# Widening block 1's narrow matmuls and transposes with zeros to the whole array

## The chip, the cores and the metric

The kernel runs on one core of a Trainium2 chip. The metric is the device time of one execution in microseconds (us): the median of three runs is given, and one further execution was profiled. TensorE's array has 128 rows and 128 columns; a matmul names the rows (partitions of its operands) and columns (of its weights) that it uses. In the rows below `64*128 64x272` means 64 rows and 128 columns of weights, and 272 columns that stream past them.

## What is computed

Two blocks work on 512 tokens of 1024 features. Only block 1 is touched. It has two layers over L = 528 tokens (16 learned ones ahead of the 512); each layer has a mixer of two branches, retention and attention, followed by a feed-forward part.

```
q_r, k_r, v_r, g_r, q_a, k_a, v_a, gate_r, gate_a = split(rms_norm(h) @ w_in)
# retention, 8 heads, 64 features to a key, 128 to a value, both directions
s = (q_c @ k_c.T) * decay_in          # within a block of 128 tokens
o = s @ v + q_dec @ state             # and over the blocks before and after
state = state * chunk_decay + k_dec.T @ v
# attention, 8 heads in 2 groups of 4, 64 features; a band of 3 blocks and the 16 first tokens
p = softmax([q @ meta_k.T, q @ k_band.T, sink]);  o = p @ [meta_v, v_band]
```

Block 2 (a gated delta rule, a linear recurrence, attention into a memory and product-key experts) follows and stays as it is.

## The kernel before

Products with weights are made in three passes of the type float32r, whose operands are split into a first part (`whi`, `uh`) and a rest (`wlo`, `ul`); they go through `gemm` (L263) in two halves of 264 tokens, or of 512 columns where layer 1 leaves the first tokens out. Other products are plain float32, which TensorE runs as two instructions to a matmul; so L767's four matmuls stand as eight in the trace. Transposes are matmuls against `ident`.

Phase A of a layer starts with the tokens' scales: sums of squares, a power on GpSimd (`rsqrt_small`, L222), transposes that spread it as rows (L375), then rope tables times these scales (L592, L593), the retention's queries and keys (L597 to L601) and the values, turned token-major by five transposes to a tile (L632). The first 16 tokens' values lie in `Vm`: the retention's in rows 0 to 15, the attention's (`VAm`) in rows 32 to 47, and, as eight small copies issued by ScalarE's queue (L657), in rows 64 to 127 again, block diagonal over the four heads of a group (`VMB`).

Then three generators are interleaved: `retention` (one head after another), `projections` (the remaining products with weights, in steps of 12 matmuls, which fill in) and `attention` (one block of queries and one group after another, two steps to a turn). They start in this order, and attention starts when its queries and keys are there. The order on each engine follows the order of this code and what the framework's scheduler makes of it.

Narrow products stand in these places:

- `scores`, L833 and L834: a head's scores are two products into the same place. `QS` holds a group's first parts in 64 rows and the rests in the other 64, `KH` the keys' first parts twice, so L833 uses all 128 rows. L834 multiplies the first parts with the keys' rests, `KL`, in the 64 rows of the group alone. Where the first 16 tokens do not lie beside the band, both are made once for 16 columns and once for the band.
- `turned`, L857, and `weighted`, L881: the weights over the first 16 tokens of four heads are turned (64 columns) and multiplied with `VMB` (64 rows).
- `retention`: L764 (16 columns), L765 (16 rows, 64 columns) and, among the outputs, L788 for the first block (16 rows, `Vm`).
- L632's first transpose to a tile, and L738 (16 columns).

Of the kernel before, what the change touches and what calls it, by code (L numbers as in the profile page):

```python
# [15 lines left out]
EPS = 1e-6  # L16
# [169 lines left out]
def _program(tc, I, out, dbg, upto, layers, pools):  # L186
# [26 lines left out]
    warm = cst.tile([128, 1], F32, name="warm")  # L213
    nc.scalar.activation(warm, ones, AF.Copy)
# [4 lines left out]
    def rsqrt_small(dst, src, scale):  # L219
        """dst = (src*scale + EPS)^-0.5 for a narrow [p, n]."""  # L220
# [6 lines left out]
    def load_w(src=None, sub=None, pool=None, into=None):  # L227
        """a tile of weights, as the sum of two that a pass each carries"""
# [85 lines left out]
    # ---------------------------------------------------------------- first block  # L314
# [42 lines left out]
    def cols6(acc, scale):  # L357
        """rsqrt(mean over partitions) per token, blocks of tokens as columns"""
# [8 lines left out]
    def bcast6(r6):  # L367
        """the same as rows, all partitions alike: slices of the tokens and where they are"""
# [26 lines left out]
    def cols(acc, scale, n):  # L395
        """rsqrt(mean over partitions) per token, [128, n/128]"""
# [7 lines left out]
    def bcast(r):  # L404
        """[128, k] -> rows [128, k*128] in PSUM, the same on all partitions"""
# [20 lines left out]
    # the memory's keys and values, a tile at a time where the first block leaves the tensor engine room  # L426
# [4 lines left out]
    mcol = cst.tile([128, 2], F32, name="mcol")  # L431
# [27 lines left out]
    def memory_values(ng, mem):  # L459
        """two steps"""  # L460
# [19 lines left out]
    # the first layer's input, and its first products  # L480
# [7 lines left out]
    def products_aside(feed_c, n, scale=1.0, fills=(), room=None):  # L488
        """the first four tiles of a phase, put aside until the tokens' scales are there"""
# [27 lines left out]
    for l in range(layers):  # L517
# [3 lines left out]
        # from here on the last layer leaves the first tokens out, except as keys and values  # L521
# [5 lines left out]
        # ============================================================ phase A  # L527
# [10 lines left out]
        # distances: between tokens of a block, and down a column to the block's ends  # L538
# [9 lines left out]
        nex = pa.tile([128, 16], F32, name="nex")  # L548
        nc.vector.tensor_scalar(nex, ex, -1.0, None, op0=OP.mult)
        # decays of a block's keys towards its end and its start, and of a whole block (of the sums from the  # L550
        # tokens before in the upper half, from those after in the lower)
# [6 lines left out]
        # what turns the distances' decays into those to a block's ends  # L558
        tdec = pa.tile([128, 2, 8], F32, name="tdec")
        for k in range(2):  # L560
            nc.vector.tensor_scalar(tdec[:, k], nex[:, 8 * k:8 * k + 8], dcol[:, 3 + k:4 + k], None, op0=OP.mult)
        # the tokens' scales as columns, for the blocks of TB
# [8 lines left out]
        Vx = R("R2", [128, 4, D], F32, "Vx")  # L571
        Vm = pa.tile([128, D], F32, name="Vm")
        VAx = pa.tile([128, 4, 128], F32, name="VAx")
        VAm = Vm[32:32 + NM, :128]
        # the attention's keys, split in two: the first parts of a group twice, the rests once
        KH = pa.tile([128, 2, L], F32R, name="KH")
        KL = pa.tile([128, L], F32R, name="KL")
        QO = R("R6", [128, 2, 4, L], F32, "QO")
        # a block of queries makes room for its own outputs; the other half holds what retention cycles through
        QA = OA = QO[:, 0]  # L580
        spare = QO[:, 1].rearrange("p a b -> p (a b)")
        # keys of one head of a chunk, with zeros for the other; a head's queries with both decays
# [7 lines left out]
        def scaled(tab):  # L590
            """a table times the tokens' scales"""
# [34 lines left out]
        # values, turned to token-major; the retention's minus their mean over a head's features, so that  # L626
        # its outputs have mean zero
        def values(m, z):
            pt, pm = PS(), PS()
            for i, (s0, n) in enumerate(TB):  # L630
                o = pm[:n, :128] if i == 0 else pt[:, 128 * i - 128:128 * i]
                nc.tensor.transpose(o, z[:, s0:s0 + n], ident)  # L632
# [19 lines left out]
        # the first tokens' values of a group, block diagonal over its heads  # L652
        VMB = Vm[64:, :512].rearrange("p (g d) -> p g d", g=2)
        nc.vector.memset(VMB, 0.0)
        for g in range(2):
            for r in range(4):
                nc.scalar.dma_start(VMB[16 * r:16 * r + 16, g, 64 * r:64 * r + 64], VAm[:, 64 * g:64 * g + 64])  # L657
# [11 lines left out]
        # ---- projections that fill in: queries and keys of the attention, then the retention's gates  # L669
        def projections():  # L670
            for c in range(5):
# [5 lines left out]
                else:  # L677
                    rope([(z, slice(0, 128))], z, rope_a, ROT_A)
                    for g in range(2):
# [3 lines left out]
                        nc.vector.tensor_tensor(KL[own], z[own], KH[own, g].bitcast(F32), op=OP.subtract)  # L683
# [11 lines left out]
        # ---- retention: within a block of tokens as it stands, between blocks by the decayed sums of keys  # L695
        # times values over the blocks before and after
        def retention():
# [35 lines left out]
            def turn(c):  # L733
                """a chunk's keys, token-major"""
# [3 lines left out]
                nc.tensor.transpose(pm[:NM, :128], QK[:, 1, c, :NM], ident)  # L738
                return pt, pm

            def decayed(h, pt, pm):
                f = slice(64 * (h % 2), 64 * (h % 2) + 64)
                kd = pa.tile([128, 576], F32, name="kd", tag="kd", bufs=2)
                k4, k0 = b4(kd[:, :512]), kd[:NM, 512:]
# [3 lines left out]
                nc.scalar.activation(k0, pm[:NM, f], AF.Copy, scale=kdec[:NM, 2, h:h + 1])  # L748
                return k4, k0
# [3 lines left out]
            for h in range(8):  # L753
# [5 lines left out]
                (k4, k0), S_, vh = kds[e], SD[e], slice(h * 128, h * 128 + 128)  # L759
# [8 lines left out]
                sT = pa.tile([128, L], F32, name="sT", tag="sT", bufs=1)  # L768
# [1190 lines left out]
```

## Time and profile before

| What | before |
|---|---|
| median of 3 runs | 3728.36 us (3717.03 to 3739.03) |
| span of the profiled execution | 3726.1 us |
| TensorE busy (its weight loads) | 3586.0 us, 96% (3212.1 us, 86%) |
| VectorE, ScalarE, GpSimd busy | 2413.2, 1494.8 and 946.7 us |
| mean granted TensorE clock | 0.976 of full speed |

The profiled execution gives its span, from the first to the last instruction; its own time is not listed apart from that, and the median of the runs lies 2.3 us above it. The ends of matmuls are modelled, so a busy TensorE need not be one that streams data all the time: the starts of successive matmuls tell more. Phase A's interleaved part lies at about 124 to 350 us in layer 0, and at about 1098 to 1300 us in layer 1; attention takes part from 184 and from 1160 us on.

### The profile page before, as it was taken

The numbers are of one execution on the slowest core, as the hardware profiler recorded it, in microseconds if no ns is written. First come the engines' busy times: TensorE is split into PE (matmuls) and PEld (weight loads), VectorE is DVE, ScalarE is ACT, GpSimd is POOL, SyncE is SP. The second block draws the span as 40 slices with busy tenths as digits, with TensorE's granted clock in tenths as the row PEclk, the third lists the DMA queues.
The fourth block names the chain that finished last, engine by engine and source line by source line (L and its number), as shares of the span: only waits on it lengthen the run. The fifth ranks groups of instructions, "written<-read, shape, count | busy, mean of one in ns | idle before, by whom it ended". The sixth has DMA issues, their size and how long they took to land. (4 is left out here: it accounts for less than half of the span.)

```text
span 3726.1 us, 54318 instructions
## 1 busy us (share of the span) xinstructions
PE 3586.0 (96%) x21341; PEld 3212.1 (86%) x21341; DVE 2413.2 (65%) x4258; ACT 1494.8 (40%) x2675; POOL 946.7 (25%) x708
## 2 busy tenths in 40 slices
PE   8999999999999999999999999997889999999998
PEld 8989999999997888788878877887778999999987
DVE  7554436333656454633467755689979988888875
ACT  4454324222444432422344453425553434434333
POOL 4211112000422111200032330446433334333321
PEclk9988999999998999999999999998999999999999
DMA  4101232222320033322232131323468878888855
GB/s 138 58 23 41 93 119 97 90 89 89 124 86 29 30 105 116 101 96 96 93 123 68 35 96 55 116 86 119 130 209 323 338 304 320 315 320 324 317 212 181
DMA packets 185887, 531.42 MB, mean 143 GB/s; under 512 B 16416, under 2 KB 70048, under 8 KB 168992
## 3 DMA queue, kind: packets, MB, share of 16 engines
q1 hardware_dynamic: 150272, 367.67, 29.6%
q0 software_dynamic: 18432, 134.23, 9.1%
q10 hardware_dynamic: 16928, 26.06, 2.1%
q8 instruction: 168, 2.75, 0.3%
q14 instruction: 87, 0.71, 0.1%
HBM read 492.64 MB, written 35.19 MB: 142 GB/s over the span
## 5 line engine op out<-in xcount | busy, mean ns | idle before, releaser
L243 ACT ACTIVATE whi<-wraw 128x1024 fp32r<-128x1024 f32 x594 | 627.6, 1058 | 1043.0 <-PE g L263 628.3
L244 DVE TENSOR_TENSOR wlo<-wraw,whi 128x1024 fp32r<-128x1024 f32 x543 | 680.5, 1254 | 294.9 <-ACT whi L243 287.6
L263 PE MATMUL g<-uh,whi 128*128 128x264 f32 (+1 forms) x1864 | 476.1, 318 | 4.6 <-ACT z L605 4.6
L263 PE MATMUL g<-uh,wlo 128*128 128x264 f32 (+1 forms) x1864 | 468.7, 314 | 1.3 <-DVE wlo L244 1.3
L263 PE MATMUL g<-ul,whi 128*128 128x264 f32 (+1 forms) x1864 | 468.8, 314 | 0.0
L350 POOL TENSOR_TENSOR ssq<-ssq,sq 128x512 f32<-128x512 f32 (+2 forms) x84 | 133.4, 1588 | 926.1 <-issue 715.8
L1721 PE MATMUL f<-TH,wlo 128*128 128x384 f32 x1024 | 348.8, 341 | 5.4 <-POOL wlo L244 5.4
L1721 PE MATMUL f<-TH,whi 128*128 128x384 f32 x1024 | 350.8, 343 | 1.2 <-ACT stash L1722 1.1
L1721 PE MATMUL f<-TL,whi 128*128 128x384 f32 x1024 | 347.5, 339 | 0.0
L263 PEld LDWEIGHTS g<-uh,whi 128*128 128x128 f32 x1864 | 308.4, 192 | 25.4 <-ACT z L605 5.0
L263 PEld LDWEIGHTS g<-uh,wlo 128*128 128x128 f32 x1864 | 307.7, 191 | 21.4 <-DVE wlo L244 1.6
L263 PEld LDWEIGHTS g<-ul,whi 128*128 128x128 f32 x1864 | 308.2, 191 | 19.6 <-issue 1.3
L1904 POOL COPY pace<-al 1x1 f32<-1x1 f32 x128 | 109.4, 855 | 563.6 <-DVE al L332 561.8
L1883 PE MATMUL acc<-whi,ah 128*128 128x512 f32 x768 | 240.1, 394 | 7.3 <-ACT whi L243 6.4
L1883 PE MATMUL acc<-wlo,ah 128*128 128x512 f32 x768 | 238.9, 392 | 4.1 <-DVE wlo L244 4.1
L1883 PE MATMUL acc<-whi,al 128*128 128x512 f32 x768 | 238.5, 392 | 0.0
L263 PE MATMUL g<-Hh,wlo 128*128 128x264 f32 (+1 forms) x768 | 203.9, 320 | 0.0
L263 PE MATMUL g<-Hl,whi 128*128 128x264 f32 (+1 forms) x768 | 203.8, 320 | 0.0
L263 PE MATMUL g<-Hh,whi 128*128 128x264 f32 (+1 forms) x768 | 203.4, 319 | 0.0
L1853 POOL DMA_INDIRECT gtile<-in_uv_dram,ix x128 | 189.8, 1483 | 46.4 <-issue 27.4
L1721 PEld LDWEIGHTS f<-TH,whi 128*128 128x128 f32 x1024 | 196.2, 192 | 5.8 <-ACT stash L1722 1.9
L1721 PEld LDWEIGHTS f<-TH,wlo 128*128 128x128 f32 x1024 | 195.5, 191 | 6.4 <-POOL wlo L244 6.4
(588 smaller groups left out, 7608.3 us busy)
## 6 DMA issues: line engine op xcount, KB each, us to landing
wraw<-in_w_dram SPq DMA_DIRECT2D x340, 512.0 KB, 3.5
wraw<-in_uT_dram SPq DMA_DIRECT2D x128, 512.0 KB, 5.6
wraw<-in_uv_dram SPq DMA_DIRECT2D x128, 512.0 KB, 4.9
gd<-stg SPq DMA_DIRECT2D x12, 2048.0 KB, 9.9
gin<-gd SPq DMA_DIRECT2D x32, 768.0 KB, 11.2
h0c<-in_h_dram SPq DMA_DIRECT2D x8, 264.0 KB, 4.3
H<-in_h_dram ACTq DMA_DIRECT2D x8, 264.0 KB, 5.9
hs<-H ACTq DMA_DIRECT2D x8, 264.0 KB, 2.1
```

Of the source, the lines that this page charges most:

```text
L243: nc.scalar.activation(hi, raw, AF.Copy)
L244: (sub or nc.vector).tensor_tensor(lo, raw, hi.bitcast(F32), op=OP.subtract)
L263: nc.tensor.matmul(pw, wt[:, sl], xt[:, kc, hf * w_:(hf + 1) * w_], start=(first and n == 0 and a == 0), stop=(last and n == len(kcs) - 1 ...
L350: nc.gpsimd.tensor_tensor(self.acc, self.acc, t, op=OP.add)
L1721: nc.tensor.matmul(p[:, :NT], wt[:, sl], x[:, kc], start=(kc == 0 and a == 0), stop=(kc == 7 and a == 2))
L1853: nc.gpsimd.indirect_dma_start(out=gtile, out_offset=None, in_=I["uv"], in_offset=bass.IndirectOffsetOnAxis(ap=ix[:, k:k + 1], axis=0))
L1883: nc.tensor.matmul(accs[2 * n + q], x[:, tk], wt[:, 512 * q:512 * q + 512], start=(j == 0 and k == 0), stop=(j == 127 and k == 2))
L1904: after = nc.gpsimd.tensor_copy(pace, ready[2][0:1, 0:1].bitcast(F32)).ins
```

## The change

Narrow operands are widened with zeros, so that the products use all 128 rows, and columns where it can be done, of the array. `KL` becomes two tiles, one for each group, with zeros in the other 64 rows (the second one takes the buffer of `ssq`). `Vm` is zeroed once and read in all its rows, against `K0`, `sT` and `pM`, which have zeros where they meet rows that belong to something else. `K0` takes the place of the part of `kd` that held the decayed keys of the first tokens; it holds both heads of a chunk side by side. `sams` are two tiles with zeros in columns 0 to 63 instead of one narrow tile. Transposes of 16 columns take 128. Some small tiles are merged (`warm`, `nex`); comments are removed, which shifts the line numbers.

```diff
         Vm = pa.tile([128, D], F32, name="Vm")
+        nc.gpsimd.memset(Vm, 0.0)
-        KL = pa.tile([128, L], F32R, name="KL")
+        KL = [pa.tile([128, L], F32R, name="KL"), wk.tile([128, L], F32R, name="KL1", tag="ssq", bufs=1)]
+        for t in KL:
+            nc.gpsimd.memset(t.bitcast(F32), 0.0)
+        sams = [pa.tile([128, 128], F32, name=f"sam{e}") for e in range(2)]
+        for e in range(2):
+            nc.gpsimd.memset(sams[e], 0.0)
+        nc.gpsimd.memset(K0, 0.0)
+        sT = pa.tile([128, L], F32, name="sT")
+        nc.gpsimd.memset(sT[:, :NM], 0.0)
...
-                o = pm[:n, :128] if i == 0 else pt[:, 128 * i - 128:128 * i]
-                nc.tensor.transpose(o, z[:, s0:s0 + n], ident)
+                o = pm[:, :128] if i == 0 else pt[:, 128 * i - 128:128 * i]
+                nc.tensor.transpose(o, z[:, s0:s0 + 128], ident)
...
-                        nc.vector.tensor_tensor(KL[own], z[own], KH[own, g].bitcast(F32), op=OP.subtract)
+                        nc.vector.tensor_tensor(KL[g][own], z[own], KH[own, g].bitcast(F32), op=OP.subtract)
...
-                nc.tensor.transpose(pm[:NM, :128], QK[:, 1, c, :NM], ident)
+                nc.tensor.transpose(pm[:, :128], QK[:, 1, c, :128], ident)
...
-                nc.scalar.activation(k0, pm[:NM, f], AF.Copy, scale=kdec[:NM, 2, h:h + 1])
+                nc.scalar.activation(K0[:NM, f], pm[:NM, f], AF.Copy, scale=kdec[:NM, 2, h:h + 1])
...
-                nc.tensor.matmul(px_[:NM, 128:128 + NM], KP[e][:, :NM], QK[:, 0, c, :NM], start=True, stop=True)
-                nc.tensor.matmul(px_[:64, :128], k0, Vm[:NM, vh], start=True, stop=True)
+                nc.tensor.matmul(px_[:, 128:128 + NM], KP[e][:, :128], QK[:, 0, c, :NM], start=True, stop=True)
+                nc.tensor.matmul(px_[:, :128], K0, Vm[:, vh], start=True, stop=True)
...
-                nc.scalar.activation(S_[:64, 1], px_[:64, :128], AF.Copy)
+                nc.scalar.activation(S_[:64, 1], px_[64 * e:64 * e + 64, :128], AF.Copy)
...
-                    nc.tensor.matmul(o, v_rows(b)[:n, vh], sT[:n, s0:s0 + n], start=True, stop=False)
+                    nc.tensor.matmul(o, v_rows(b)[:, vh], sT[:, s0:s0 + n], start=True, stop=False)
...
-                    nc.tensor.matmul(sp[:nq, a:a + n], QS[own, g, r], KL[own, b:b + n], start=False, stop=True)
+                    nc.tensor.matmul(sp[:nq, a:a + n], QS[:, g, r], KL[g][:, b:b + n], start=False, stop=True)
...
-            nc.gpsimd.tensor_copy(sam[:nq], sa[:nq, :, 0:16])
+            sam = sams[g]
+            nc.gpsimd.tensor_copy(sam[:nq, 64:].rearrange("p (r k) -> p r k", r=4), sa[:nq, :, 0:16])
...
-            nc.tensor.transpose(pm[:64, :nq], sam[:nq], ident[:nq, :nq])
+            nc.tensor.transpose(pm[:, :nq], sams[g][:nq], ident[:nq, :nq])
-            nc.vector.tensor_copy(pM[64:, :nq], pm[:64, :nq])
+            nc.vector.tensor_copy(pM[:, :nq], pm[:, :nq])
...
-            nc.tensor.matmul(po[:nq, :256], pM[64:, :nq], VMB[:, g], start=True, stop=False)
+            nc.tensor.matmul(po[:nq, :256], pM[:, :nq], VMB[:, g], start=True, stop=False)
```

The order of instructions moves in few places. Here is TensorE's at the start of layer 0's retention, head 0 (the shape is that of the result; L765 is the product of the first tokens' keys and values, L767 those of the blocks, L788 the first block's output). Before:

```order
L263 MATMUL g<-uh,wlo 128x264 x2
L767 MATMUL s<-Vx,kd 128x128
L765 MATMUL s<-Vm,kd 64x128
L767 MATMUL s<-Vx,kd 128x128 x3
L263 MATMUL g<-uh,whi 128x264 x2
L263 MATMUL g<-ul,whi 128x264 x2
```

And with the change, where L776 is what L765 was, and L778 what L767 was (`Vx` as its second name is `K0`, which lies in the same tile):

```order
L263 MATMUL g<-uh,wlo 128x264 x2
L778 MATMUL s<-Vx,kd 128x128 x4
L263 MATMUL g<-uh,whi 128x264 x2
L776 MATMUL s<-Vm,Vx 128x128
L263 MATMUL g<-ul,whi 128x264 x2
```

The product with `Vm` moved behind all four of the blocks and two of the filling matmuls, since it reads all rows of `Vm`.

GpSimd's order at the start of layer 1's phase A (L222 is the power of the tokens' scales, the SD tiles are the retention's sums). Before:

```order
L543 IOTA dcol 128x1 x5
L588 MEMSET SD_10308 128x640
L222 TENSOR_TENSOR r_10244<-r_10244,mhalf 88x6
L588 MEMSET SD_10309 128x640
L593 TENSOR_TENSOR rope_r<-rope_r,rsb 128x528
```

And with the change:

```order
L542 IOTA dcol 128x1 x5
L574 MEMSET Vm 128x1024
L222 TENSOR_TENSOR r_10236<-r_10236,mhalf 88x6
L581 MEMSET KL 128x528
L581 MEMSET KL_10299 128x528
L585 MEMSET sam_10302 128x128
L585 MEMSET sam_10303 128x128
L589 MEMSET sT 128x16
L600 MEMSET SD_10311 128x640
L600 MEMSET SD_10312 128x640
L605 TENSOR_TENSOR rope_r<-rope_r,rsb 128x528
```

`Vm`'s memset stands where one of SD's stood, and five more stand between the power and the rope table's scaling, beside both of SD's.

## Rows read from the trace of the kernel before

**Rows 1.** The page: the span.

```profile
span 3726.1 us, 54318 instructions
```

**Rows 2.** Busy time by stretch: retention alone and with attention, layers 0 and 1.

```profile
core 0: us, PE busy (x) PEld busy (x) DVE busy (x) ACT busy (x) POOL busy (x), PEclk, DMA share, GB/s
124.00:184.00 60.00, 56.22 (x468) 53.15 (x466) 37.23 (x78) 24.38 (x66) 22.34 (x16) 1.00 0.16 51
184.00:350.00 166.00, 165.55 (x1055) 141.15 (x1056) 79.25 (x244) 79.33 (x192) 23.85 (x26) 0.86 0.07 23
1098.00:1160.00 62.00, 59.31 (x459) 55.66 (x458) 37.52 (x75) 23.47 (x63) 21.37 (x16) 0.94 0.15 51
1160.00:1300.00 140.00, 138.43 (x770) 109.06 (x770) 72.12 (x209) 72.03 (x168) 20.80 (x24) 0.89 0.07 22
```

**Rows 3.** TensorE's waits, 184 to 350 us: total, times, longest.

```profile
PE s L833 <- ACT KH L682: 1.5, 1, 1.5
```

**Rows 4.** TensorE's timeline, 233.4 to 237 us: start, duration, engine, line, operation.

```profile
233.40 0.42 PE L263 MATMUL g<-uh,wlo 128*128 128x264 f32 x2
233.65 0.34 PE L833 MATMUL s<-KH,QS 128*128 128x400 f32 x1
...
234.30 0.45 PE L833 MATMUL s<-KH,QS 128*128 128x400 f32 x1
234.68 0.45 PE L834 MATMUL s<-KL,QS 64*128 64x400 f32 x1
235.06 0.45 PE L833 MATMUL s<-KH,QS 128*128 128x400 f32 x1
```

**Rows 5.** TensorE's timeline, 219 to 222 us.

```profile
219.54 0.59 PE L833 MATMUL s<-KH,QS 128*128 128x272 f32 x1
220.06 0.59 PE L834 MATMUL s<-KL,QS 64*128 64x272 f32 x1
...
221.19 0.64 PE L263 MATMUL g<-ul,whi 128*128 128x264 f32 x2
221.63 0.64 PE L263 MATMUL g<-uh,wlo 128*128 128x264 f32 x2
```

**Rows 6.** The tile KL: its products, count and forms.

```profile
L834 PE MATMUL s<-KL,QS x104: 273/386/699, 184.8 to 1281.0; 64*128 64x16 f32 x32, 64*128 64x272 f32 x16, 64*128 64x400 f32 x16, 64*128 64x384 f32 x16
```

**Rows 7.** TensorE's timeline, 130 to 138 us, without the lines of L263.

```profile
130.78 0.43 PE L765 MATMUL s<-Vm,kd 16*64 16x128 f32 x2
...
135.01 0.43 PE L765 MATMUL s<-Vm,kd 16*64 16x128 f32 x2
135.36 0.94 PE L767 MATMUL s<-Vx,kd 128*128 128x128 f32 x6
136.13 0.29 PE L789 MATMUL g<-QO,SD 128*128 128x16 f32 x2
136.28 0.47 PE L788 MATMUL g<-sT,Vx 128*128 128x128 f32 x2
```

**Rows 8.** The tile Vm: its products, and its copies from issue to landing.

```profile
L881 PE MATMUL s<-Vm,pM x36: 376/480/792, 199.0 to 1297.9; 64*128 64x256 f32 x32, 64*16 64x256 f32 x4
L765 PE MATMUL s<-Vm,kd x32: 267/293/318, 130.8 to 1266.5; 16*64 16x128 f32 x32
L788 PE MATMUL g<-sT,Vm x32: 257/278/392, 132.6 to 1286.0; 16*128 16x16 f32 x32
...
DMA to landing us min/median/max: 1.6/1.8/2.2
```

**Rows 9.** GpSimd's groups by form: busy us, mean ns.

```profile
L585 POOL MEMSET QO<- 128x2112 f32 x2 | 3.7, 1867 | 3.9 <-DVE tn L1046 3.9
```

**Rows 10.** TensorE's timeline, start of layer 1's phase A.

```profile
1010.11 0.67 PE L375 MATMUL s<-ident,r 88*128 88x88 f32 x6 [1.05 <-POOL r L222]
```

**Rows 11.** ScalarE's timeline, issues of the copies into Vm.

```profile
126.21 3.18 ACTq L657 DMA_DIRECT2D Vm<-Vm  x5
```

**Rows 12.** Busy time by stretch, around a fall of the clock (columns as in rows 2).

```profile
199.40:202.80 3.40, 3.40 (x29) 2.64 (x29) 2.14 (x8) 2.34 (x4) 1.31 (x1) 1.00 0.02 5
...
216.50:223.30 6.80, 6.80 (x25) 5.37 (x24) 2.54 (x12) 1.87 (x5) 1.50 (x2) 0.50 0.00 1
```

More of the change, by code (lines that the diff above doesn't have):

```diff
@@ L212, in _program @@
     nc.vector.memset(ones, 1.0)
-    warm = cst.tile([128, 1], F32, name="warm")
-    nc.scalar.activation(warm, ones, AF.Copy)
+    mcol = cst.tile([128, 2], F32, name="mcol")
+    nc.scalar.activation(mcol[:, 0:1], ones, AF.Copy)
     mhalf = cst.tile([128, 8], F32, name="mhalf")
@@ L430, in _program @@
     ghead = cst.tile([128, 8], F32, name="ghead")
-    mcol = cst.tile([128, 2], F32, name="mcol")
     mrow = []
@@ L547, in _program @@
             nc.scalar.activation(ex, ex, AF.Exp)
-        nex = pa.tile([128, 16], F32, name="nex")
-        nc.vector.tensor_scalar(nex, ex, -1.0, None, op0=OP.mult)
+        nex = pa.tile([128, 8], F32, name="nex")
+        nc.vector.tensor_scalar(nex, ex[:, :8], -1.0, None, op0=OP.mult)
         kdec = pa.tile([128, 4, 8], F32, name="kdec")
@@ L560, in _program @@
         for k in range(2):
-            nc.vector.tensor_scalar(tdec[:, k], nex[:, 8 * k:8 * k + 8], dcol[:, 3 + k:4 + k], None, op0=OP.mult)
+            nc.vector.tensor_scalar(tdec[:, k], ex[:, 8 * k:8 * k + 8], dcol[:, 3 + k:4 + k], -1.0, op0=OP.mult, op1=OP.mult)
         rcol = pa.tile([128, 5], F32, name="rcol")
@@ L570, in _program @@
         QK = R("R3", [128, 2, 4, L], F32, "QK")
-        Vx = R("R2", [128, 4, D], F32, "Vx")
+        Vx_ = R("R2", [128, 4 * D + 128], F32, "Vx")
+        Vx, K0 = Vx_[:, :4 * D].rearrange("p (b d) -> p b d", b=4), Vx_[:, 4 * D:]
         Vm = pa.tile([128, D], F32, name="Vm")
+        nc.gpsimd.memset(Vm, 0.0)
         VAx = pa.tile([128, 4, 128], F32, name="VAx")
@@ L651, in _program @@
         values(*turned_)
-        VMB = Vm[64:, :512].rearrange("p (g d) -> p g d", g=2)
-        nc.vector.memset(VMB, 0.0)
+        VMB = Vm[:, :512].rearrange("p (g d) -> p g d", g=2)
+        nc.vector.memset(VMB[64:], 0.0)
         for g in range(2):
             for r in range(4):
-                nc.scalar.dma_start(VMB[16 * r:16 * r + 16, g, 64 * r:64 * r + 64], VAm[:, 64 * g:64 * g + 64])
+                nc.scalar.dma_start(VMB[64 + 16 * r:80 + 16 * r, g, 64 * r:64 * r + 64], VAm[:, 64 * g:64 * g + 64])
         rope_a = pa.tile([128, 2, L], F32, name="rope_a", tag="rope")
@@ L742, in decayed @@
                 f = slice(64 * (h % 2), 64 * (h % 2) + 64)
-                kd = pa.tile([128, 576], F32, name="kd", tag="kd", bufs=2)
-                k4, k0 = b4(kd[:, :512]), kd[:NM, 512:]
+                k4 = b4(pa.tile([128, 512], F32, name="kd", tag="kd", bufs=2))
                 src = pt.rearrange("p (b d) -> p b d", b=4)[:, :, f]
@@ L747, in decayed @@
                 nc.scalar.activation(k4[:, :, 64:], src, AF.Copy, scale=kdec[:, 1, h:h + 1])
-                nc.scalar.activation(k0, pm[:NM, f], AF.Copy, scale=kdec[:NM, 2, h:h + 1])
-                return k4, k0
+                nc.scalar.activation(K0[:NM, f], pm[:NM, f], AF.Copy, scale=kdec[:NM, 2, h:h + 1])
+                return k4
             T = prepare(0)
@@ L758, in retention @@
                     yield
-                (k4, k0), S_, vh = kds[e], SD[e], slice(h * 128, h * 128 + 128)
+                k4, S_, vh = kds[e], SD[e], slice(h * 128, h * 128 + 128)
                 st, px_, pu = PS(), PS(), PS()
@@ L763, in retention @@
                                      start=True, stop=True)
-                nc.tensor.matmul(px_[:NM, 128:128 + NM], KP[e][:, :NM], QK[:, 0, c, :NM], start=True, stop=True)
-                nc.tensor.matmul(px_[:64, :128], k0, Vm[:NM, vh], start=True, stop=True)
+                nc.tensor.matmul(px_[:, 128:128 + NM], KP[e][:, :128], QK[:, 0, c, :NM], start=True, stop=True)
+                nc.tensor.matmul(px_[:, :128], K0, Vm[:, vh], start=True, stop=True)
                 for b in range(4):
                     nc.tensor.matmul(pu[:, 128 * b:128 * b + 128], k4[:, b], Vx[:, b, vh], start=True, stop=True)
-                sT = pa.tile([128, L], F32, name="sT", tag="sT", bufs=1)
                 nc.vector.tensor_tensor(b4(sT[:, NM:]), b4(st), T[:, None, :].to_broadcast([128, 4, 128]), op=OP.mult)
                 nc.vector.tensor_mul(sT[:NM, :NM], px_[:NM, 128:128 + NM], T[:NM, :NM])
-                nc.scalar.activation(S_[:64, 1], px_[:64, :128], AF.Copy)
+                nc.scalar.activation(S_[:64, 1], px_[64 * e:64 * e + 64, :128], AF.Copy)
                 nc.scalar.activation(S_[64:, 3], pu[64:, 384:], AF.Copy)
@@ L815, in scores @@
             q0, nq = TB[qb]
-            own = slice(64 * g, 64 * g + 64)
             if qb == 0:
@@ L848, in scores @@
             nc.vector.reciprocal(den, den)
-            sam = wk.tile([128, 4, 16], F32, name="sam", tag="sam", bufs=1)
-            nc.gpsimd.tensor_copy(sam[:nq], sa[:nq, :, 0:16])
-            return qb, g, ot, kb, sa, den, sam
+            sam = sams[g]
+            nc.gpsimd.tensor_copy(sam[:nq, 64:].rearrange("p (r k) -> p r k", r=4), sa[:nq, :, 0:16])
+            return qb, g, ot, kb, sa, den
         def turned(u):
-            qb, g, ot, kb, sa, den, sam = u
+            qb, g, ot, kb, sa, den = u
             q0, nq = TB[qb]
             pm = PS()
-            nc.tensor.transpose(pm[:64, :nq], sam[:nq], ident[:nq, :nq])
+            nc.tensor.transpose(pm[:, :nq], sams[g][:nq], ident[:nq, :nq])
             pM = wk.tile([128, 128], F32, name="pM", tag="tm", bufs=3)
-            nc.vector.tensor_copy(pM[64:, :nq], pm[:64, :nq])
+            nc.vector.tensor_copy(pM[:, :nq], pm[:, :nq])
             pTs = []
@@ L876, in weighted @@
         def weighted(u, pM, pTs):
-            qb, g, ot, kb, sa, den, sam = u
+            qb, g, ot, kb, sa, den = u
             q0, nq = TB[qb]
```

## The prediction

> **What bounds the kernel now.** I read the page's span first, then a table of stretches, then the waits of TensorE, then the timeline of TensorE inside those stretches. The profiled execution spans 3726.1 us [rows 1]; the median of the three runs, 3728.36, lies 2.3 us above it, so I take the sum off the median. The change touches only phase A of both layers of block 1: the retention alone, and then retention, attention and the filling projections in turns. There the reader is to see two things in the stretches [rows 2]. TensorE counts as busy nearly all the time (165.55 of 166 us in layer 0, 138.43 of 140 in layer 1), while VectorE and ScalarE are each busy for about half (79.25 and 79.33 of 166). And the granted clock falls to 0.86 and 0.89 in the attention stretches and to 0.94 in layer 1's retention. TensorE has one wait of 1.5 us in the whole 166 us of layer 0's attention [rows 3]. So TensorE's own order sets the end there: what is taken off it comes off the time until VectorE or ScalarE cannot follow.
>
> Busy is not useful, though. In the timeline, two matmuls of 264 columns over the whole array start 0.25 us apart as a pair, 0.125 each. Scores run as KH (128 rows), KL (64 rows), KH, KL; each has 400 columns, so by columns each should take 0.19. They start 0.38 apart, in both directions [rows 4]. The 0.19 us over belongs to each passage between a 128-row and a 64-row product; an ordinary change of weights, as between the 264-column products, has no such gap. At half the clock the same pattern of 272 columns takes 0.52 a product, where two of 264 take 0.44 together, 0.22 each: 0.29 over [rows 5, 12].
>
> **The change part by part.**
>
> *The rests of the scores (KL).* There are 104 such products, 32 of 16 columns [rows 6]; each has a passage into it and one out. With zeros in the other 64 rows they have the same shape as KH, so the passages go. 72 long ones x 2 x 0.19 = 27.4 us. A short one gains less: two whole-array products of 16 columns (L789) take 0.15 together, 0.075 each [rows 7], where their columns would need under 0.01, so some 0.06 of the 0.19 stays. I take 32 x 2 x 0.13 = 8.3 us (0 to 12.2). At half the clock a passage costs 0.10 more; some 28% of layer 0's attention ran there (below), 144 x 0.28 x 0.10 = 4.0. Together 40 us.
>
> *The narrow float32 products* (L881 x36, L765 x32, L788 with Vm x32 [rows 8]) stand in pairs, two passes to a matmul: 50 pairs. An L765 pair takes 0.35, then six whole ones take 0.77, 0.128 each, 0.26 a pair [rows 7]. The least a pair gains is thus 0.09; the most is 0.09 and one passage, 0.28. I take 0.20: 50 x 0.20 = 10 us (4.5 to 14).
>
> *Narrow columns.* L764, L738, the first transpose of `values` and `sam`'s gain columns of weights only. L764 is the one with a short moving side, so the weight load could show: at most the price of a whole 16-column pair, 0.15 [rows 7], for each of 16 pairs, 2.4 us; nothing if the load lies under the product before. The others stream 128 columns before and after. I take +1 (0 to 2.4). By the Trainium skill ("TensorE: Matmul & The Clock Gate", LDWEIGHTS), a load takes its columns over 1.2 ns, so 112 more columns would be 93 ns on each of 32 loads, an estimate of 3.0 us if nothing hid them.
>
> *Zeros.* They are written once a layer, on POOL. The heaviest is Vm, 1024 columns; QO's 2112 take 1.87, so 0.9 us [rows 9]. In layer 1 it stands right ahead of the scales' power (L222), for which TensorE waited 1.05 us [rows 10]; before, an SD memset stood there, so at most 0.9 is added. KL's two, sT's and the two SD come behind the power and ahead of the rope; in layer 0 one KL memset stands ahead of the power. I take 1 us for both layers (0 to 3).
>
> *A new wait.* K0 x Vm (L776) now reads all of Vm, so also the rows that eight small ACT-issued copies fill. The last five issues end at 129.39 in layer 0, landing takes 1.8 us from issue, so it lands by about 131.2 at the latest. L765 ran at 130.78 [rows 7, 8, 11]. Behind it on TensorE stand head 0's other products. +0.4 a layer, 0.8 in all (0 to 3).
>
> *The clock.* Time at half the clock is twice the missing share: 166 x 0.14 x 2 = 46.5, 62 x 0.06 x 2 = 7.4, 140 x 0.11 x 2 = 30.8, together 85 us [rows 2]. At 216.5 to 223.3 the granted clock is 0.50, that is 1.2 GHz; at 199.4 to 202.8, ahead of its fall, it was still the full 2.4 GHz [rows 12], and TensorE ran products one by one, KH and KL and other short ones, with their passages between. Some 12 us of the 85 are passages at half clock (counted above), so 73 us of work would shrink to 36.5 if the full clock always held. It will still fall after real stalls (the start of attention, the wait on POOL), so I take a little over half: -20 (0 to -36).
>
> *Waits that surface.* With 59 to 70 us less on TensorE over two layers, VectorE and ScalarE go from 48% busy to about 60% in layer 0 (79 of 132). The in-order chain scores, maximum, exponentials, transposes then shows up now and then on TensorE. No row has such a wait now; between 0 and 10 us a layer as an estimate from these shares, and I take 4 a layer: +8.
>
> Sum: -40 -10 +1 +1 +0.8 -20 +8 = -59 us, 3728.4 - 59 = **3669 us** (a span of about 3667).
>
> **The rivals.**
>
> *The clock comes back whole.* If dense scores keep the full clock everywhere, -50 +3 -36 +4 = -79: 3649 us. For it: every other dense stretch of the block runs at full clock, as layer 0's retention does at 1.00 [rows 2]. Against: waits stay that have nothing to do with the passages.
>
> *Another engine takes the bound.* VectorE's maximum over each score, ScalarE's exponentials and table loads share one chain. If half of the gain turns into waits for them: -50 +3 -5 +25 = -27: 3701 us. For it: both already work half the time in a stretch that shortens by a fifth. Against: they wait for TensorE now, TensorE not for them [rows 3].
>
> *The gap is not the passage.* If 0.19 us belongs to the scores as such (the accumulation into one bank, the load of QS a second time), only the additions stay: +3, 3731 us. Against: float32 pairs of another kind show a gap too, and KL to KH is as slow as KH to KL, while QS's load is hidden elsewhere.
>
> *Slower: narrow products now run beside their neighbours, and wide ones could not.* Then each widened product would add its own streaming: KL's 104 have 23,552 columns (the 24 not listed have 256), at 0.125 us for 264 that is 11.1 us; L881 36 x 0.256 = 9.2, L765 32 x 0.128 = 4.1, L788 32 x 0.075 = 2.4; with the additions +30: 3758 us. It decides only if more than half of the narrow products overlap today. Against: no KL starts less than 0.38 after a long KH in [rows 4], so nothing runs beside it. By the Trainium skill ("TensorE: Matmul & The Clock Gate", Part 3: Packing small matmuls — row/col tiling) products on distinct groups of rows start within about 4 ns of each other, and a weight load overlaps a running matmul only when the rows differ; by that rule this change would be a loss. The trace disagrees here, for the neighbours of the narrow product are whole-array ones; its page "TensorEngine Tiling (Array Packing)", Key Properties, says that changing the tiling mode drains the engine, with no price, and that is what 0.19 us looks like.
>
> **How the numbers follow.** Forecast 0.54, whole clock 0.20, another bound 0.16, not the passage 0.06, side by side 0.04. The lowest that I can justify is all bounds at their best short of none of the waits, about -90, 3638; the high end takes in the case of another bound and its scatter, 3705. That leaves out the last two cases and the tails, under 2 in 10. A change under 0.5% (18.6 us, 3709.7) is about what a measurement of this kernel cannot tell from none; the three runs lie within 0.3% of their median. Faster by more: all of the first two and three quarters of the third, 0.86. Within: the rest of the third and the fourth, 0.10. Slower: 0.04.
>
> **What would show it.** Right: KH and KL of 400 columns start about 0.19 us apart, 272 columns about 0.13; the two attention stretches together shorten by 50 us or more, and nothing outside phase A moves by more than a few us; the granted clock in them is above 0.93. The clock term is wrong if it stays below 0.90 there; the waits term is wrong if TensorE's waits in one attention stretch exceed 10 us. The passage is wrong if products of equal shape still start 0.38 apart. The additions are wrong if head 0's K0 product waits more than 1.5 us for a DMA, or TensorE waits over 2 us for POOL's power at a layer's start.

## The result and the profile after

The changed kernel takes **3663.91 us** (median of 4 runs, 3659.06 to 3670.65) beside 3728.01 us before (4 runs, 3717.03 to 3739.03): a ratio of 0.983, interval 0.981 to 0.986. It is 64 us faster; 59 were forecast.

The busy time by stretch of the changed kernel, cut at the first retention product, the first score and the last finish of the attention of each layer (us, PE, PEld, DVE, ACT, POOL busy, granted clock, DMA share, GB/s):

```profile
span 3660.7 us, 54336 instructions
126.72:184.43 57.71, 52.55 (x454) 51.65 (x454) 40.58 (x78) 23.11 (x59) 21.01 (x16) 1.00 0.15 47
184.43:307.20 122.77, 122.51 (x1042) 119.04 (x1043) 73.91 (x243) 77.14 (x188) 24.91 (x26) 1.00 0.10 31
1061.16:1119.01 57.85, 52.84 (x442) 51.11 (x442) 40.70 (x77) 23.24 (x56) 21.02 (x16) 1.00 0.16 47
1119.01:1230.44 111.43, 109.31 (x782) 99.20 (x783) 69.83 (x209) 69.94 (x165) 21.62 (x23) 0.98 0.09 30
sum 349.76, PE 337.21 PEld 321.00 DVE 225.02 ACT 193.44 POOL 88.56; mean PE 84.30 PEld 80.25 DVE 56.26 ACT 48.36 POOL 22.14
```

The kernel before, cut at the same landmarks (the cuts of [rows 2] lie a little outside them):

```profile
184.30:348.40 164.10, 163.95 (x1043) 139.55 (x1043) 77.51 (x243) 77.45 (x188) 23.85 (x26) 0.85 0.07 23
1162.30:1302.20 139.90, 139.66 (x781) 110.48 (x782) 71.02 (x209) 70.20 (x165) 20.70 (x23) 0.89 0.07 24
sum 423.90, PE 416.02 PEld 355.68 DVE 224.37 ACT 194.16 POOL 88.37; mean PE 104.01 PEld 88.92 DVE 56.09 ACT 48.54 POOL 22.09
```

The two attention stretches lost 41.3 and 28.5 us, with the same number of matmuls (1043 and 1042, 781 and 782) and the same work on VectorE and ScalarE. All of phase A lost 74.1. The granted clock, 0.85 and 0.89 there, is 1.00 and 0.98: almost the full 2.4 GHz all the way.

What [rows 4] showed at 0.38 us from start to start now reads as follows (start, duration, engine, line, operation; L842 is the old L833, L843 the old L834):

```profile
205.59 0.29 PE L842 MATMUL s<-KH,QS 128*128 128x272 f32 x1
...
205.71 0.29 PE L843 MATMUL s<-KL,QS 128*128 128x272 f32 x1
...
217.15 0.34 PE L842 MATMUL s<-KH,QS 128*128 128x400 f32 x1
217.16 0.19 PEld L843 LDWEIGHTS s<-KL,QS 128*128 128x128 f32 x1
217.34 0.34 PE L843 MATMUL s<-KL,QS 128*128 128x400 f32 x1
217.34 0.19 PEld L842 LDWEIGHTS s<-KH,QS 128*128 128x128 f32 x1
217.52 0.34 PE L842 MATMUL s<-KH,QS 128*128 128x400 f32 x1
...
217.71 0.34 PE L843 MATMUL s<-KL,QS 128*128 128x400 f32 x1
```

Starts lie 0.18 to 0.19 us apart for 400 columns, 0.12 for 272 (205.59 to 205.71): what the columns need at the 0.125 us that 264 columns take in [rows 4]. The reader should also see the weight loads (PEld): that of the next product starts together with the product before it (217.16 beside 217.15, 217.34 beside 217.34), so that load and product overlap.

TensorE's waits in three stretches, 120 to 330 us (layer 0's phase A), 900 to 1061 us (ahead of layer 1's retention) and 1000 to 1240 us (layer 1's phase A): total, times, longest.

```profile
PE s L375 <- POOL r L222: 3.0, 2, 2.0
PE s L842 <- ACT KH L694: 1.8, 1, 1.8
PE s L776 <- ACT Vx L759: 0.4, 1, 0.4
...
PE s L375 <- POOL r L222: 0.9, 1, 0.9
...
PE s L375 <- POOL r L222: 3.0, 2, 2.0
PE s L842 <- DVE QS L821: 1.6, 1, 1.6
PE s L773 <- DVE sm L844: 0.8, 1, 0.8
PE s L873 <- DVE pM L868: 0.5, 1, 0.5
PE s L866 <- DVE sm L857: 0.5, 1, 0.5
```

In the kernel before, 120 to 350 us and 1000 to 1305 us (the latter with the 1.05 us of [rows 10]):

```profile
PE s L375 <- POOL r L222: 2.3, 3, 1.3
...
PE s L375 <- POOL r L222: 3.5, 3, 2.1
...
PE s L833 <- DVE QS L811: 1.3, 1, 1.3
```

The wait for KH in layer 0 stood before as well, with 1.5 us [rows 3], and that for QS in layer 1 with 1.3; new on the attention's chain are the last three rows of the first list, 1.8 us in both layers together, and 0.3 more on either of those two. The waits for GpSimd's power beside the retention (L375) grew too, from 2.3 and 2.4 to 3.0 and 3.0. VectorE and ScalarE did not become the bound.

### The profile page after: what moved, and what is told of

Same layout as the page of the kernel before. It is cut to its first block, busy times and chain, and to the rows that moved or that the text cites. A ratio compares the mean times of both kernels' runs of the same rounds, so it can differ in the third digit from the quotient of the medians.

```text
span 3660.7 us, 54336 instructions
## 1 busy us (share of the span) xinstructions
PE 3516.7 (96%) x21341; PEld 3187.1 (87%) x21341; DVE 2413.3 (66%) x4258; ACT 1494.5 (41%) x2675; POOL 954.5 (26%) x722
## 5 line engine op out<-in xcount | busy, mean ns | idle before, releaser
L263 PE MATMUL g<-uh,whi 128*128 128x264 f32 (+1 forms) x1864 | 470.9, 315 | 4.4 <-ACT z L617 3.2
L263 PE MATMUL g<-uh,wlo 128*128 128x264 f32 (+1 forms) x1864 | 465.0, 312 | 1.3 <-DVE wlo L244 1.3
L263 PE MATMUL g<-ul,whi 128*128 128x264 f32 (+1 forms) x1864 | 465.3, 312 | 0.0
L263 PEld LDWEIGHTS g<-uh,whi 128*128 128x128 f32 x1864 | 305.2, 189 | 23.9 <-ACT z L617 3.6
L263 PEld LDWEIGHTS g<-uh,wlo 128*128 128x128 f32 x1864 | 305.0, 189 | 20.1 <-DVE wlo L244 1.5
L263 PEld LDWEIGHTS g<-ul,whi 128*128 128x128 f32 x1864 | 305.2, 189 | 17.9
L263 PE MATMUL g<-Hh,wlo 128*128 128x264 f32 (+1 forms) x768 | 204.0, 320 | 0.0
L263 PE MATMUL g<-Hl,whi 128*128 128x264 f32 (+1 forms) x768 | 203.8, 320 | 0.0
L263 PE MATMUL g<-Hh,whi 128*128 128x264 f32 (+1 forms) x768 | 203.4, 319 | 0.0
```

Source lines behind the costliest of these rows:

```text
L263: nc.tensor.matmul(pw, wt[:, sl], xt[:, kc, hf * w_:(hf + 1) * w_], start=(first and n == 0 and a == 0), stop=(last and n == len(kcs) - 1 ...
```

## The experiments

**Only KL widened.** Of the change, the kernel before takes KL alone.

```diff
-        KL = pa.tile([128, L], F32R, name="KL")
+        KL = [pa.tile([128, L], F32R, name="KL"), wk.tile([128, L], F32R, name="KL1", tag="ssq", bufs=1)]
+        for t in KL:
+            nc.gpsimd.memset(t.bitcast(F32), 0.0)
...
-                    nc.tensor.matmul(sp[:nq, a:a + n], QS[own, g, r], KL[own, b:b + n], start=False, stop=True)
+                    nc.tensor.matmul(sp[:nq, a:a + n], QS[:, g, r], KL[g][:, b:b + n], start=False, stop=True)
```

> The kernel before with KL alone widened (two zero-padded tiles, 104 products of 128 rows instead of 64); the float32 products and all narrow columns stay. If the score rests carry the gain and the clock: passages of KL gone, about 28 us at full clock, and the half-clock time of phase A (84 us of matmul starts in the trace before) down to under 15 us, so 3665 to 3680. If the float32 narrow products hold the clock down as well: passages alone, 3690 to 3705, with the granted clock of the two attention stretches still under 0.93.

Measured: 3679.12 us (3676.18 to 3681.28), ratio 0.986, interval 0.984 to 0.989: 51 us of the whole change's 64. Its attention stretches:

```profile
185.28:312.63 127.35, 127.11 (x1041) 118.34 (x1042) 76.35 (x243) 77.17 (x188) 24.15 (x26) 1.00 0.10 30
1124.96:1239.17 114.21, 112.60 (x781) 96.76 (x782) 71.21 (x209) 69.92 (x165) 20.73 (x23) 1.00 0.09 29
```

The clock is 1.00 in both, with all the narrow float32 products still there. So the falls of the clock went with KL's passages; the other narrow products alone do not bring the clock down.

**All but KL.** The changed kernel with the KL products narrow again.

```diff
-        KL = [pa.tile([128, L], F32R, name="KL"), wk.tile([128, L], F32R, name="KL1", tag="ssq", bufs=1)]
-        for t in KL:
-            nc.gpsimd.memset(t.bitcast(F32), 0.0)
+        KL = pa.tile([128, L], F32R, name="KL")
...
-                    nc.tensor.matmul(sp[:nq, a:a + n], QS[:, g, r], KL[g][:, b:b + n], start=False, stop=True)
+                    nc.tensor.matmul(sp[:nq, a:a + n], QS[own, g, r], KL[own, b:b + n], start=False, stop=True)
```

> The changed kernel with KL alone narrow again (64 rows, as before); everything else wide. If the score rests carry the gain: only about 10 us of the float32 products are kept, 3710 to 3724, granted clock in the attention stretches still 0.86 to 0.90. If the float32 products matter as much: under 3700.

Measured: 3715.55 us (3712.37 to 3721.99), ratio 0.996, interval 0.995 to 0.997: 15 us of the gain is left. With the run before, 51 + 15 = 66, beside 64 for the whole change (and 66 for the run with narrow columns below, measured beside the same runs of before): the two parts add up. The attention stretches:

```profile
184.73:332.82 148.09, 147.97 (x1042) 132.02 (x1043) 75.07 (x243) 77.43 (x188) 24.11 (x26) 0.93 0.08 26
1143.31:1275.61 132.30, 131.18 (x781) 108.78 (x782) 71.20 (x209) 70.13 (x165) 20.80 (x23) 0.92 0.08 25
```

The clock, 0.93 and 0.92, lies above the 0.86 to 0.90 that I had expected: beside KL's passages the other narrow products may have a share in its falls.

**Fewer passages, same products.** In the kernel before, the scores of two heads are taken together, KH KH KL KL in place of KH KL KH KL. Every product keeps its shape; where the array changed between 128 and 64 rows once a product, it now changes every second one. In TensorE's order as it came out, KL stands in 68 runs in place of 102, so a third of KL's passages go, not half.

```diff
-            for r in range(4):
-                sp = PS()
-                for a, b, n in segs:
-                    nc.tensor.matmul(sp[:nq, a:a + n], QS[:, g, r], KH[:, g, b:b + n], start=True, stop=False)
-                    nc.tensor.matmul(sp[:nq, a:a + n], QS[own, g, r], KL[own, b:b + n], start=False, stop=True)
...
+            for r0 in (0, 2):
+                sps = [PS(), PS()]
+                for a, b, n in segs:
+                    for k, sp in enumerate(sps):
+                        nc.tensor.matmul(sp[:nq, a:a + n], QS[:, g, r0 + k], KH[:, g, b:b + n], start=True, stop=False)
+                    for k, sp in enumerate(sps):
+                        nc.tensor.matmul(sp[:nq, a:a + n], QS[own, g, r0 + k], KL[own, b:b + n], start=False, stop=True)
...
```

> The kernel before, all products narrow as they were, but the scores of two heads in the order KH, KH, KL, KL; TensorE's order then has 68 runs of KL instead of 102, so 68 passages fewer. If the gap belongs to the passage between 128-row and 64-row products: KL after KL and KH after KH of 400 columns 0.17 to 0.19 us apart, 0.38 only where the rows change; 10 to 13 us less from the passages and up to as much again from the clock, 3702 to 3718. If the gap belongs to the score products as such (accumulation, the second load of QS, or 64 rows being slow): 0.38 between all of them, and 3728 within a few us.

Measured: 3703.63 us (3699.88 to 3712.04), ratio 0.993, interval 0.991 to 0.995. Not one zero was added and no product widened, and 27 us went. By the price below, 68 passages fewer are worth 13 us at full clock; the granted clock, 0.93 and 0.95 between 184.5 and 340 and between 1150 and 1290 us, gave back more. So the price belongs to the change between narrow and whole-array products, and not to the narrow product as such. This order also takes two products into the same place apart; but in the changed kernel they still follow each other, and no gap is there. TensorE's timeline (L834 is KH, L836 KL; each row is two products; in brackets the idle time ahead, in which the load waited for nothing that the profile shows):

```profile
244.14 0.32 PEld L834 LDWEIGHTS s<-KH,QS 128*128 128x128 f32 x2
244.26 0.53 PE L834 MATMUL s<-KH,QS 128*128 128x400 f32 x2
244.72 0.29 PEld L836 LDWEIGHTS s<-KL,QS 64*128 64x128 f32 x2 [0.26 <-issue]
244.72 0.63 PE L836 MATMUL s<-KL,QS 64*128 64x400 f32 x2
245.27 0.30 PEld L834 LDWEIGHTS s<-KH,QS 128*128 128x128 f32 x2 [0.26 <-issue]
...
245.84 0.29 PEld L836 LDWEIGHTS s<-KL,QS 64*128 64x128 f32 x2 [0.27 <-issue]
```

Four products take 1.12 us (244.72 to 245.84), 0.56 a pair, where two of [rows 4] took 0.76 and two of the changed kernel take 0.37. So each pair pays 0.19 once, where before each product did. The weight loads tell what is paid for: at a passage the load does not start under the product before, PEld stands idle for 0.26 us, and load and product then begin together. The starts from product to product show the price in two halves. For 400 columns at full clock (two to four of each) they are: KH to KH behind a passage 0.286 to 0.290 and KH to KL 0.275 to 0.277, KL to KL 0.285 to 0.290 and KL to KH 0.271 to 0.272, each about 0.1 over the 0.18 that the columns need. Where I had expected the second KL to follow the first within 0.17 to 0.19, it did not; the total was as expected. By the Trainium skill ("TensorEngine Tiling (Array Packing)", Key Properties) a change of the tiling mode drains the engine. The idle 0.26 us of PEld agrees with that.

**Narrow columns alone put back.** The changed kernel, with the first transpose of `values`, L738's transpose and L764 (the changed kernel's L775) back to 16 columns.

```diff
-                nc.tensor.matmul(px_[:, 128:128 + NM], KP[e][:, :128], QK[:, 0, c, :NM], start=True, stop=True)
+                nc.tensor.matmul(px_[:NM, 128:128 + NM], KP[e][:, :NM], QK[:, 0, c, :NM], start=True, stop=True)
```

(and the two transposes likewise)

> The changed kernel with the narrow columns of L632's first transpose, L738 and L764 put back (16 columns of weights, 128 rows). If a change of columns alone costs nothing and a load of 128 columns shows under a 16-column product: 1 to 2 us less than the changed kernel, 3660 to 3665, not to be told from it by the time; the pairs of that product 0.04 us a product faster. If columns make a passage too: 34 products more with two passages each, 5 to 13 us more, 3669 to 3677.

Measured: 3664.70 us (3658.88 to 3668.46), ratio 0.983, interval 0.980 to 0.985, the same as the change. Fewer columns of weights make no passage; that part of the change is worth nothing that the time shows. L775 by itself took 99 ns from start to start in the mean, beside 113 in the changed kernel: 14 ns, where I had expected 40.

**A narrow product beside a narrow one.** In the kernel before, each KL product is followed by an additional product over the other 64 rows, into a PSUM tile of its own.

```diff
-                sp = PS()
+                sp, s2 = PS(), PS()
...
                     nc.tensor.matmul(sp[:nq, a:a + n], QS[own, g, r], KL[own, b:b + n], start=False, stop=True)
+                    nc.tensor.matmul(s2[:nq, a:a + n], QS[oth, g, r], KH[oth, g, b:b + n], start=True, stop=True)
```

> The kernel before, in which each KL product (64 rows of one half) is followed at once by one more narrow product, over the other 64 rows and as many columns (QS times KH of the other half, into a PSUM tile of its own that nothing reads). So its time holds work that the reference doesn't need, and it tells of the rate alone. Passage theory (whole-array and narrow products exclude each other, and a narrow pair has a price at its two ends): the added product is narrow as well, so it adds a narrow product's own time and no further passage: starts from the KL product to the added one lie 0.17 to 0.29 us apart at 400 columns, 0.12 to 0.20 at 272, and the attention stretches grow by 15 to 30 us each time 104 is spread over both layers (about 104 times 0.17, 18 us in all). Side-by-side theory (two narrow products on different rows run together): the added product starts at most 0.03 us behind the KL product, and the stretches grow by less than 6 us in all.

Measured, in one execution: 3743.72 us, beside 3727.65 before (3721.67 to 3732.81). TensorE's timeline (L833 KH, L834 KL, L835 the added product):

```profile
238.61 0.45 PE L833 MATMUL s<-KH,QS 128*128 128x400 f32 x1
...
238.99 0.18 PEld L834 LDWEIGHTS s<-KL,QS 64*128 64x128 f32 x1 [0.20 <-issue]
239.00 0.44 PE L834 MATMUL s<-KL,QS 64*128 64x400 f32 x1
239.00 0.18 PEld L835 LDWEIGHTS s<-KH,QS 64*128 64x128 f32 x1
239.00 0.45 PE L835 MATMUL s<-KH,QS 64*128 64x400 f32 x1
...
239.37 0.19 PEld L263 LDWEIGHTS g<-uh,whi 128*128 128x128 f32 x1 [0.20 <-issue]
239.38 0.39 PE L263 MATMUL g<-uh,whi 128*128 128x264 f32 x1
```

My passage theory, as I had written it, is wrong on one point. The added product starts with KL's (3 to 4 ns behind by the starts, in 78 of the 85 pairs in which it is the next to start): two narrow products on different rows do run side by side. Its attention stretches:

```profile
184.30:356.50 172.20, 172.16 (x1098) 145.88 (x1099) 79.17 (x243) 80.02 (x190) 25.91 (x26) 0.83 0.07 22
1166.90:1309.30 142.40, 141.77 (x829) 110.83 (x830) 71.16 (x209) 70.31 (x165) 22.13 (x23) 0.90 0.07 23
```

These two grew by 10.6 us, between the under 6 of the one theory and the 15 to 30 of the other. Phase A grew by 8 us in all beside the first profile of before, which has about the same time at half clock (by 19 beside the second, which has less, below). Of the 8, KL and the added products together account for 5.6 (40.1 us from start to start, KL alone 34.5 before); by columns alone, one after the other, they would have added 11, an estimate from 264 columns in 0.125 us. Where those 5.6 come from, I did not resolve. What the theory needs held all the same: from KH to KL is 0.39 us and from the narrow pair to L263 0.38, with the same idle 0.20 ahead of both loads. So a narrow product can share the array with a narrow one; in none of these rows does it share it with a whole-array one.

**Half of KL.** The changed kernel with KL narrow for the second group of heads only: 52 of 104.

```diff
+            rows = slice(64 * g, 128)
...
-                    nc.tensor.matmul(sp[:nq, a:a + n], QS[:, g, r], KL[g][:, b:b + n], start=False, stop=True)
+                    nc.tensor.matmul(sp[:nq, a:a + n], QS[rows, g, r], KL[g][rows, b:b + n], start=False, stop=True)
```

> The changed kernel with the KL products of the second group of heads narrow again (64 rows), the first group's as changed: half of the 104 passages. Bounds from runs already made: 3664 (none narrow) and 3716 (all narrow). Passages alone, at a full clock: 0.5 times 28.5 us, 3678. If the clock follows the passages evenly, half of the remaining 23 us as well: 3690 (3685 to 3695), with some 20 us of half clock in the four stretches of phase A (3.6 and 40.5 us at the ends). If the clock falls only beyond some density of passages: 3678 (3674 to 3683), and under 8 us of half clock. Theory that the whole effect lies in the first passages (the clock falls as soon as any are there): above 3700, over 30 us of half clock.

Measured: 3691.02 us (3688.31 to 3691.84), ratio 0.990, interval 0.988 to 0.992: halfway between none narrow (3664) and all narrow (3716). The attention stretches:

```profile
183.20:318.70 135.50, 135.36 (x1041) 125.94 (x1042) 74.77 (x243) 77.45 (x188) 24.82 (x26) 0.96 0.09 28
1131.70:1254.50 122.80, 121.53 (x782) 104.68 (x783) 71.49 (x209) 70.14 (x165) 21.23 (x23) 0.94 0.09 27
```

Time at half clock, twice the missing share as in the prediction, is 135.5 x 0.04 x 2 + 122.8 x 0.06 x 2 = 26 us here, 42 with all KL narrow, 4 with none (one execution each). The median times, 3664, 3691 and 3716 us, are even as well: with none, 52 and 104 narrow KL products the clock goes down step by step, as I had expected. Together with the other narrow products (the kernel before) it is 85 in one execution and 58 in another (below), with those alone none. So it is not the count of changes by itself: in the order of starts the run with KL alone widened still has some 70 changes between narrow and whole-array products in its attention stretches and no time at half clock, this run some 110 and 26 us.

**Both kernels once more**, unchanged, for the scatter of what lies outside phase A.

> The kernel before once more, unchanged, for a second profile. Outside phase A (from the start to the first retention product, between the two layers' phases A, and from the last finish of the attention to the end) its first profile has 2576.1 us, the changed kernel's 2584.2 and six others' 2580 to 2590, though the code there is the same. If that is the scatter of single executions: 2579 to 2590 us here. If the change (or a shorter phase A) costs time elsewhere: 2573 to 2578 us again.

> The changed kernel once more, unchanged, for a second profile beside it. If the 8 us more outside phase A are scatter: anything from 2575 to 2590 us outside, and phase A at 350 us (349.8 in its first profile) with under 8 us of half clock. If they are caused by the change: 2582 to 2587 us outside, and 6 us or more above the kernel before of the same chip.

The totals "outside" in these expectations have a slip of adding: all are 600 us short (752.2 + 665.4 + 1758.5 is 3176.1, not 2576.1), and they leave out the first 126 us. Their differences stand. Measured, in one execution each: 3727.89 and 3670.16 us. Outside phase A: before 3176.1 and now 3186.8, after 3184.2 and now 3190.2. The 8 us by which the changed kernel's first profile was longer there are within the 10.7 us that the kernel before shows against itself. Phase A of the second profile of before:

```profile
184.80:340.30 155.50, 155.38 (x1041) 133.93 (x1042) 77.46 (x243) 77.23 (x188) 23.88 (x26) 0.91 0.08 25
1095.60:1154.80 59.20, 54.81 (x442) 51.00 (x442) 37.80 (x77) 23.36 (x56) 21.78 (x16) 1.00 0.14 46
...
sum 412.80, PE 404.25 PEld 347.02 DVE 223.42 ACT 193.90 POOL 88.74; mean PE 101.06 PEld 86.75 DVE 55.85 ACT 48.48 POOL 22.18
```

It is 11 us shorter than in the first one, and the clock accounts for it: 0.91 where 0.85 stood, 1.00 where 0.94 stood, so 58 us at half clock in place of 85, which is worth at most half of the 27 us between them. The changed kernel's second phase A has 351.0 us against 349.8, with 7 us at half clock. So phase A gained 74 us by the first pair of profiles and 62 by the second; the median's 64 lies in between, and a single profile of before is good to some 10 us here.

## Why the prediction was right

The predicted 3669 us was 5 above the measured median, by a mechanism that held. That it came as close as 5 us is partly luck: the score products gained less than predicted, and less was lost to waits. The terms, as predicted and as measured (mean from a matmul's start to the next one's, at full clock, over phase A of both profiles, times the count; a wait ahead of a product lies within its mean, so the fourth and the fifth row are no terms of their own in the right column; the predicted -40 holds 4 us for passages at half clock, which on the right lie in the last row):

```
term                        predicted   measured
KL and KH, 104 each            -40      -28.5   (KH 277 -> 154 ns, KL 289 -> 138 ns)
narrow float32 products        -10      -12     (L881 310 -> 226, L765 179 -> 141, all of L788 129 -> 113, and neighbours)
narrow columns                  +1       +1.3   (L764 73 -> 113 ns, x31)
zeros, K0's wait on copies      +1.8     +0.7   (within: L776 0.3 and 0.4)
waits that surface              +8       +3.7   (within; 1.3 of it for GpSimd's power)
clock                          -20      -22 to -35
```

The run with KL alone widened bears out the second row another way: its phase A has 359.8 us where the changed kernel has 349.8, and no time at half clock where that has 4. Of the +1.3 in the third row the columns themselves make 0.4 (the 14 ns of the run with narrow columns, x31); the rest came with L764's neighbours.

*The passage.* Right in its cause, by the runs with only KL, without KL, with half of KL and above all with two heads together, which leaves all shapes as they were. That refutes "the gap is not the passage", and the loss by "side by side" as well: the changed kernel would have had to be slower. By the Trainium skill ("TensorE: Matmul & The Clock Gate", Part 3: Packing small matmuls — row/col tiling) products on distinct groups of rows start within about 4 ns; the trace agrees where both are narrow (3 to 4 ns); beside a whole-array product no row here shows it (0.38 and 0.39 us from start to start). The rule on weight loads that the prediction cites with it, that a load overlaps only other rows, is not what the changed kernel's rows show: there whole-array loads start together with a whole-array product (217.34).

*Its size* was the term that was off: 28.5 us at full clock where 36 were predicted. I gave each long product both of its passages at 0.19. For 400 columns that holds (medians 0.377 to 0.183, both KH and KL). But 32 of the 72 long products come right behind two of 16 columns, and there a whole-array stream is not free of gaps either. The changed kernel's timeline:

```profile
261.72 0.17 PE L842 MATMUL s<-KH,QS 128*128 128x16 f32 x1
...
261.74 0.26 PE L843 MATMUL s<-KL,QS 128*128 128x16 f32 x1
261.83 0.19 PEld L842 LDWEIGHTS s<-KH,QS 128*128 128x128 f32 x1
261.86 0.42 PE L842 MATMUL s<-KH,QS 128*128 128x384 f32 x1
261.94 0.19 PEld L843 LDWEIGHTS s<-KL,QS 128*128 128x128 f32 x1
262.12 0.34 PE L843 MATMUL s<-KL,QS 128*128 128x384 f32 x1
...
262.29 0.17 PE L842 MATMUL s<-KH,QS 128*128 128x16 f32 x1
```

KH of 384 columns is followed after 0.26 us, KL of 384 after 0.17. Before, both stood at 0.37: one gained 0.11, the other 0.19. I read it as the weight load that two products of 16 columns are too short to cover (the loads at 261.83 and 261.94 start 0.11 apart); no run takes it apart. That makes some 2.6 us of the shortfall; the rest is spread over the other KH and the products of 16 queries. The 16-column ones gained a little less than predicted (0.13 for KH and 0.09 for KL).

*The clock.* I took a little over half of what a full clock would give, since I expected it to fall again after the stalls that stay. It did not: 4 and 7 us of half clock are left in the two profiles of phase A, and none with KL alone widened. The rival "the clock comes back whole" had this term right; its 3649 us is 15 too low, for it took 50 us for the passages, where 40 were measured at full clock. What it is worth depends on the execution of before that one compares with: phase A was shorter by 62 or by 74 us, of which the first three rows are 39, so 22 to 35. That the clock falls with KL's passages is shown by the runs with 0, 52 and 104 narrow KL products (4, 26 and 42 us of half clock, and their medians); why it falls is not.

*The other engines.* "Another engine takes the bound" is refuted by the 2.4 us of new waits on the attention's chain: 63% busy for ScalarE and 60% for VectorE (77 and 74 of 123 us) was not enough to hold TensorE up, and +8 was too much.

*Additions.* Vm's zeros stand ahead of the power, and cost nothing there: TensorE waits 0.9 us for it in layer 1, where it waited 1.05 [rows 10]. The product with K0 waits 0.4 us, but for ScalarE's writing of K0 (L759) and not for a copy: other products were put ahead of it, so that it starts at 132.3 in layer 0, and by the 1.8 us that a copy takes from issue the last of them had landed before. Both stay under the bounds that the prediction named.

## What to carry over

Where narrow matmuls alternate with whole-array ones, look at the distance from start to start, not at busy time: a change between them cost 0.195 us at full clock here for products of 400 columns, whichever way it goes, and less for short ones. Widening with zeros adds no moving columns; where that can't be done, put narrow products in runs, which here gave 27 us. Two on different rows side by side would save changes as well; no run here tried that on products that are needed. And such a stream may give back a second time through the granted clock, which one can't read from a single profile of the kernel before: take two.

## What the runs showed of the hardware that I had not expected

- A passage shows on both of its sides: the product ahead of it is left about 0.1 us late (KL to KH 0.27 where 0.18 was due), the next load starting only after it, and so is the product behind it (KL to KL 0.29).
- Two products on different halves of the rows run together even when they read other tiles and write other PSUM tiles (3 to 4 ns apart), and an added 104 of them cost 5.6 us. The clock was 0.83 and 0.90 with them, against 0.85 or 0.91 and 0.89 without: no difference that one execution could show.
- The pairs of narrow float32 products pay in the same two halves. L881 (64 rows, 256 columns) took 0.320 us for the first pass, behind a whole-array product, and 0.306 for the second, ahead of one, where each takes 0.215 when widened. So a pair went from 0.63 (228.72 to 229.35) to 0.43 (240.95 to 241.38). Whether a narrow pass inside a longer run of narrow ones is slower than a wide one, no run here shows.
- The same kernel granted 0.85 or 0.91 in the same stretch in two executions whose spans are both 3726.1 us.
